# Half of w2 in a wide expert block as float32 products instead of split float32r products

## The chip, the cores and the metric

One Trainium2 chip, one core of it. The metric is the time of one execution in device microseconds. The kernel is the whole trunk in one launch; its inputs lie in HBM, and its output is written back there.

## The reference

Two layers. Each has a mixer (pooling and convolution groups), a normalization, a channel mixer, a normalization and a gated embedding. The first layer's channel mixer is a dense SwiGLU; the second's is a mixture of eight experts, of which each token takes two. The change is in that second one:

```python
def swiglu(h, w1, w3, w2):
    return (jax.nn.silu(h @ w1) * (h @ w3)) @ w2
...
    for e in range(N_EXPERTS):
        out = out + gates[:, e:e + 1] * swiglu(t, w1[e], w3[e], w2[e])
```

256 tokens, width 1024, 3584 hidden units an expert, all float32.

## The kernel before, in words

**Precision.** The products are made from float32r numbers, which hold fewer bits. A weight w is split into H (a cast of w to float32r, on ACT, line 146) and L (w - H, on DVE, line 161); the data likewise into h and l. `mm` (lines 342 to 352) then makes three products, h x H (347), h x L (351) and l x H (352), in one PSUM accumulation. Four small matrices that are named in `DIRECT` (line 39) are multiplied as float32 without a split (344).

**Experts.** Each expert gathers its tokens into places: the four with most tokens ("wide", even numbers here) into 128, the other four ("narrow", odd numbers) into 64. In a narrow block h and l lie side by side in the 128 columns of the stationary operand, so two products (347, 349) do what takes three in a wide one, and a product with a shift matrix folds the two halves together (1052). An expert has seven blocks (e, c) of 512 hidden units. `BLOCKS` (line 75) lists the 56 blocks: four wide ones, then narrow and wide in turns, then four narrow ones.

**A block** in `experts` (1054 to 1138) multiplies its w1 (1070) and w3 (1084), makes the gate product g on DVE (661), and then multiplies w2 of the block before it (`down`, 1105), whose hidden units were ready. At its end a wide block turns its own g: four transposes on PE (335), a cast to gH on ACT (320) and the rest gL on DVE (321). A narrow block's g is turned in the next block, after w1 (382 for the rest).

**Weights.** w1, w3 and w2 of a block come as two transfers of 1 MB each ("halves"; 12 for a pair of blocks), issued by the SP queue (line 117). All raw halves, all H and all L lie in one pool of 19 buffers of 8 KB a partition. `Weights.advance` is called whenever PE's next half is asked for: it issues the transfers ahead, and the cast and subtraction of following halves, as long as at most `hl` = 8 buffers hold H and L that are not used up. So a cast needs two buffers, and waits for whoever used these before: a subtraction that read a raw half, or a product that read an H or an L. The order of instructions on each engine is the order in which the program writes them (manual schedule); nothing overtakes on ACT and DVE.

**Around it.** Where a wide or narrow expert ends, its sums are evacuated and scattered to the tokens (814 to 817); where one begins, its tokens are gathered (796). In block 53 a branch on the counts of tokens (1039) is passed, which every engine waits at.

The names in the pair of blocks that the text follows, in the order in which PE multiplies them: N1 to N4 are the halves of w1 and w3 of the narrow block, W1 and W2 the halves of w2 of the wide block before it, A1 to A4 the halves of w1 and w3 of the wide block, B1 and B2 those of w2 of the narrow block.

Of the kernel before, what the change touches and what calls it, by code (L numbers as in the profile page):

```python
# [10 lines left out]
F32R = mybir.dt.float32r  # L11
# [6 lines left out]
P = 128  # L18
D = 1024
# [58 lines left out]
class Weights:  # L78
# [8 lines left out]
        self.slow, self.later = set(), []  # L87
        self.temps = TEMPS_START

    def add(self, name, src, k, n, whole=False):  # L90

        direct = name in DIRECT
        m = k if direct or whole else 1024 // n
        for j in range(0, k, m):
            self.names.setdefault(name, []).append(len(self.items))
            self.items.append(dict(load=len(self.loads), at=j * n, k=m, n=n, direct=direct, done=False,
                                   slots=2 if whole else 1))
        self.loads.append((src, k * n))

    def slot(self, n, dt=F32):  # L100
# [96 lines left out]
def trunk(ctx: ExitStack, tc: tile.TileContext, a: dict, out: bass.AP):  # L197
    nc = tc.nc
# [20 lines left out]
        return ap.tile([P] + shape, dt, tag=tag, name=tag)  # L219

    W = Weights(nc, wp)
    eids, at_place = [None], {}

    def expert_at(s):
# [5 lines left out]
    for l in range(L):  # L230
        for b in range(2):
            W.add(f"wg{b}{l}", a["w_gv"][l, 0, b], KD, 256)
            W.add(f"wv{b}{l}", a["w_gv"][l, 1, b], KD, 256)
        for k in range(2):
            W.add(f"wu{l}", a["w_u"][l, :, k * 2048:(k + 1) * 2048], 4, 512)
        for c in range(2):
            W.add(f"wo0{l}", a["w_out"][l, c, :, 0:2048], 4, 512)
        W.add(f"pw{l}", a["w_small"][l, :, 0:2048], 4, 512)
        for c in range(2):
            W.add(f"wo1{l}", a["w_out"][l, c, :, 2048:4096], 4, 512)  # L240

        def up_items(tag, w1, w3, nf, whole=False):
            for t, src in (("w1", w1), ("w3", w3)):
                for b in range(0, KD * nf, 2048):
                    W.add(f"{t}{tag}", piece(src, b), 2048 // nf, nf, whole)

        def down_items(tag, w2, nf, whole=False):
            for b in range(0, nf // P * D, 2048):
                W.add(f"w2{tag}", piece(w2, b), 2, D, whole)

        def piece(src, b):
            if callable(src):
                return lambda: src()[:, b:b + 2048]
            return src[:, b:b + 2048]

        def expert(name, e, c):

            if e == 0:
                return a[name][0, c]
            return lambda: a[name][bass.ds(expert_at(e), 1), c].rearrange("o p f -> (o p) f")  # L260

        if l % 2 == 0:
            units = [(f"d{c}", a["dense_w1"][c], a["dense_w3"][c], a["dense_w2"][c], nf, False)
                     for c, (f0, nf) in enumerate(DENSE_CHUNKS)]
        else:
            units = [(f"e{e}_{c}", *(expert(name, e, c) for name in ("exp_w1", "exp_w3", "exp_w2")), 512, (e, c) != (0, 0))
                     for e, c in BLOCKS]
        for i, (tag, w1, w3, w2, nf, whole) in enumerate(units):
            up_items(tag, w1, w3, nf, whole)
            if i:  # L270
                down_items(units[i - 1][0], *units[i - 1][3:])
        down_items(units[-1][0], *units[-1][3:])
        W.add(f"ple{l}", a["ple_w"][l], 2, D)
        for c in range(2):
            for b in range(2):
                W.add(f"gate{c}{l}", a["ple_gate_w"][l, c, :, b * 2048:(b + 1) * 2048], 4, 512)
# [41 lines left out]
    def split_into(dst, src):  # L318

        nc.scalar.copy(dst.h, src)  # L320
        nc.vector.tensor_sub(dst.l, src, dst.h.bitcast(F32))  # L321
        if dst.f is not None:
            nc.scalar.copy(dst.f, src)
# [8 lines left out]
    def transposes(src, n):  # L332
        t = mmt("tr")
        for i in range(n):
            nc.tensor.transpose(t[:, i * P:(i + 1) * P], src[:, i * P:(i + 1) * P], ident)
        return bank(t, n)
# [327 lines left out]
    def hidden(g, nf, h, tags=("gH", "gL")):  # L664

        n = nf // P
        gT = Split(*(tl(f"{t}{h}", [4, P], F32R) for t in tags))
        split_into(gT[:, :n, :], transposes(g, n))
        return gT

    def hidden_narrow(g, par):
# [372 lines left out]
    def experts(ranks, gates, xr, yacc, nxt, first, more, end):  # L1044

        prev = pend = made = turn = None
        selTs, state = [nxt[0], None], {0: nxt[1:]}

        def fold(p, lo):
            nc.tensor.matmul(p, shift, lo, start=False, stop=True, skip_group_check=True)

        for i, (e, c) in enumerate(BLOCKS):
            if i == 0:
                continue
            gsl, xg = state[e]
            par = e % 2
            narrow = PLACES[e] != P
            assert narrow == (par == 1)  # L1060
            if c == 0 or i == 1:
                accs = acc("y", 2 * par), acc("y", 2 * par + 1)
                state[e, "accs"] = accs
            accs = state[e, "accs"]
            lo = tl("xL1", [2, 512], F32R) if narrow else None
            p1 = mmt("p1")
            final = i == len(BLOCKS) - 1
            if final:
                W.cap = W.names[f"w2e{prev[0]}_{prev[1]}"][1]
            both(f"w1e{e}_{c}", [p1], [xg])  # L1070
            if made is not None:
                prev[3] = made()
                made = None
            if i == 1:
                prev = [0, 0, accs, first()]
            if narrow:
                nc.scalar.copy(lo[:, 0], p1)
            else:
                s_ = silu(p1, 512, par)
            more_ = c == 3 and e + 1 < NE  # L1080
            if more_:
                xg1 = gather(sel, xr, 1 - par, (0,), None, PLACES[e + 1])
            p3 = mmt("p3")
            both(f"w3e{e}_{c}", [p3], [xg])
            if narrow:
                nc.scalar.copy(lo[:, 1], p3)
                fold(p1, lo[:, 0])
                s_ = silu(p1, 512, par)
            else:
                g = glu(s_, p3, 512, par, gsl)  # L1090
            if more_:
                gather(sel, xr, 1 - par, (1,), xg1, PLACES[e + 1])
                state[e + 1] = gate_select(sel, cc, 1 - par), xg1
            pe, pc, paccs, pgT = prev
            ids = W.names[f"w2e{pe}_{pc}"]
            if final:
                down(ids[:1], paccs, pgT, pc == 0, False, True)
                if narrow:
                    fold(p3, lo[:, 1])
                    g = glu(s_, p3, 512, par, gsl)  # L1100
                W.cap = W.names[f"w2e{e}_{c}"][-1] + 1
                W.hl = HL_PRE
                down(ids[1:], paccs, pgT, False, pc == FE - 1, True, 2)
            else:
                down(ids, paccs, pgT, pc == 0, pc == FE - 1, True)
                if narrow:
                    fold(p3, lo[:, 1])
                    g = glu(s_, p3, 512, par, gsl)
            if turn is not None:
                if pend is not None:  # L1110
                    scatter(*pend, yacc, 2 * (turn % 2))
                    pend = None
                selTs[turn % 2] = turn_select(sel, turn % 2)
                turn = None
            elif pend is not None:
                scatter(*pend, yacc, 0)
                pend = None
            if pc == FE - 1:
                pend = selTs[pe % 2], evacuate(paccs)
            if more_:  # L1120
                turn = e + 1
            prev = [e, c, accs, None]
            if not narrow:
                prev[3] = hidden(g, 512, par)
            elif final:
                prev[3] = hidden_narrow(g, par)
            else:
                made = lambda g=g, par=par: hidden_narrow(g, par)
            if i + 1 < len(BLOCKS):
                e1, c1 = BLOCKS[i + 1]  # L1130
                if c1 == 3 and e1 + 1 < NE:
                    sel, cc = select(e1 + 1, ranks, gates, 0, (e1 + 1) % 2, PLACES[e1 + 1])
            if i == MORE_AT:
                more()
            if i == len(BLOCKS) - 1 - FE:
                W.temps = TEMPS_END
            if e == NE - 1:
                end(c)
        pe, pc, paccs, pgT = prev
        down(W.names[f"w2e{pe}_{pc}"], paccs, pgT, False, True, True)  # L1140
        end(FE)
        y = evacuate(paccs)
        return lambda h: scatter(selTs[1], y, yacc, 2 * (pe % 2), (h,))
# [166 lines left out]
```

## Time and profile before

| | |
|---|---|
| median of 3 runs | 1419.0 us (1416.77 to 1420.04) |
| profiled execution | 1417.34 us |
| its span, first to last instruction | 1415.6 us |
| mean granted clock of TensorE | 0.974 |
| PE, DVE, ACT, POOL busy | 1310.6, 1199.9, 938.9, 92.3 us |
| HBM read | 430.85 MB, 305 GB/s over the span |

Busy times are of instructions on each engine; PE's matmuls are pipelined, so that a duration of 0.39 us is longer than the step from one start to the next, and steps are read from starts. An idle time in brackets stands before the row's instruction, with what ended it.

### The profile page before, as it was taken

The page shows a single profiled execution, that of the slowest core. Times are in us where ns is not written, and L with a number is a line of the kernel's source. Part 1 is how long each engine was busy: PE and PEld are TensorE (multiplying, and loading weights), DVE is VectorE, ACT ScalarE, POOL GpSimd, SP SyncE. Part 2 cuts the span into 40 slices and gives each one's busy share as a digit, 9 for nine tenths or more (in the row PEclk, how much of TensorE's full clock was granted, in tenths as well). Part 3 has the DMA queues.
Part 4 walks back from the last instruction along what each step waited for, and adds up shares of the span by engine and source line. Part 5 has one row for each costly group of instructions (what it writes and reads, how often), then busy time and mean ns, then how long its engine had stood idle before and what let it go on. Part 6 is the DMA issues. An engine that isn't in the chain of part 4 may idle for free. (4 is left out here: it accounts for less than half of the span.)

```text
span 1415.6 us, 16882 instructions
## 1 busy us (share of the span) xinstructions
PE 1310.6 (93%) x6186; PEld 1060.0 (75%) x6186; DVE 1199.9 (85%) x1082; ACT 938.9 (66%) x883; POOL 92.3 (7%) x71
## 2 busy tenths in 40 slices
PE   6769999999869999999999999999999999999877
PEld 5638888888637887777777778778777777778656
DVE  3996844557966889999999999999999999999885
ACT  4543634426533668887887787787787788788662
POOL 0430000010560200000000000000000000000000
PEclk8889999999988999999999999999999999999999
DMA  9335755427544589999999999999999999999950
GB/s 381 121 119 178 266 180 179 178 97 272 196 173 177 204 334 406 420 387 350 418 417 354 402 420 353 391 417 367 384 421 376 375 409 387 371 360 423 356 191 30
DMA packets 62170, 433.07 MB, mean 306 GB/s; under 512 B 6960, under 2 KB 7472, under 8 KB 11008
## 3 DMA queue, kind: packets, MB, share of 16 engines
q1 hardware_dynamic: 60336, 425.60, 77.0%
q0 software_dynamic: 1168, 4.23, 0.9%
q10 hardware_dynamic: 576, 2.10, 0.5%
q8 instruction: 50, 0.82, 0.2%
q14 instruction: 40, 0.33, 0.1%
HBM read 430.85 MB, written 1.05 MB: 305 GB/s over the span
## 5 line engine op out<-in xcount | busy, mean ns | idle before, releaser
L161 DVE TENSOR_TENSOR w<-w 128x2048 fp32r<-128x2048 f32 (+1 forms) x460 | 895.9, 1988 | 72.6 <-ACT w L146 61.7
L146 ACT CAST w<-w 128x2048 fp32r<-128x2048 f32 (+1 forms) x460 | 751.1, 1671 | 157.1 <-PE p L351 39.5
L347 PE MATMUL p<-w,xH 128*128 128x512 f32 (+1 forms) x1096 | 434.5, 396 | 8.8 <-DVEq L1039 5.8
L352 PE MATMUL p<-w,xL 128*128 128x512 f32 (+1 forms) x648 | 251.0, 387 | 1.3 <-DVE xL L321 1.3
L351 PE MATMUL p<-w,xH 128*128 128x512 f32 (+1 forms) x648 | 250.3, 386 | 0.4 <-DVE w L161 0.4
L347 PEld LDWEIGHTS p<-w,xH 128*128 128x128 f32 x1096 | 207.8, 190 | 50.3 <-issue 6.5
L349 PE MATMUL p<-w,xH 128*128 128x512 f32 x448 | 180.3, 402 | 16.6 <-DVE w L161 16.6
L347 PE MATMUL y<-w,gH 128*128 128x512 f32 x448 | 176.4, 394 | 1.8 <-DVE gH L382 1.6
L352 PEld LDWEIGHTS p<-w,xL 128*128 128x128 f32 x648 | 122.5, 189 | 26.7 <-DVE xL L321 1.8
L351 PEld LDWEIGHTS p<-w,xH 128*128 128x128 f32 x648 | 122.7, 189 | 24.8 <-DVE w L161 1.3
L349 PEld LDWEIGHTS p<-w,xH 128*128 128x128 f32 x448 | 85.0, 190 | 46.8 <-DVE w L161 30.7
L347 PEld LDWEIGHTS y<-w,gH 128*128 128x128 f32 x448 | 84.6, 189 | 21.0 <-DVE gH L382 2.7
L490 DVE SCALAR_TENSOR_TENSOR yc<-w,vec,yc 128x256 f32<-128x256 f32 x156 | 91.8, 661 | 0.0
L349 PE MATMUL y<-w,gH 128*128 128x512 f32 x224 | 88.4, 395 | 2.4 <-DVE w L161 2.4
L351 PE MATMUL y<-w,gH 128*128 128x512 f32 x224 | 89.7, 400 | 0.0
L352 PE MATMUL y<-w,gL 128*128 128x512 f32 x224 | 87.4, 390 | 0.0
L498 POOL TENSOR_TENSOR gH<-gH,w 128x512 f32<-128x512 f32 x38 | 66.3, 1744 | 107.9 <-ACT w L495 105.5
L429 POOL DMA_DIRECT2D w<-in_pT x2 | 1.2, 580 | 984.6 <-DVE w L161 826.2
L652 ACT ACTIVATE s<-p 128x512 f32<-128x512 f32 (+1 forms) x69 | 41.0, 596 | 28.5 <-PE p L352 28.5
L321 DVE TENSOR_TENSOR gL<-tr,gH 128x512 fp32r<-128x512 f32 x38 | 25.6, 684 | 32.6 <-ACT gH L320 32.6
L351 PEld LDWEIGHTS y<-w,gH 128*128 128x128 f32 x224 | 42.0, 188 | 14.1 <-DVE w L161 6.0
L349 PEld LDWEIGHTS y<-w,gH 128*128 128x128 f32 x224 | 42.6, 190 | 11.7 <-DVE w L161 3.0
(223 smaller groups left out, 1454.2 us busy)
## 6 DMA issues: line engine op xcount, KB each, us to landing
w<-in_exp_w SPq DMA_DIRECT2D x336, 1024.0 KB, 8.0
w<-in_dense_w SPq DMA_DIRECT2D x33, 1024.0 KB, 5.1
w<-in_w_out SPq DMA_DIRECT2D x8, 1024.0 KB, 6.5
w<-in_ple_gate_w SPq DMA_DIRECT2D x8, 1024.0 KB, 5.3
w<-in_w_gv SPq DMA_DIRECT2D x6, 1024.0 KB, 6.1
w<-in_w_u SPq DMA_DIRECT2D x4, 1024.0 KB, 9.6
w<-in_w_gv SPq DMA_DIRECT2D x4, 512.0 KB, 6.9
w<-in_w_small SPq DMA_DIRECT2D x2, 1024.0 KB, 10.2
```

The lines of the kernel that those rows point to most:

```text
L146: nc.scalar.copy(h, w)
L161: engine.tensor_tensor(l, w, h.bitcast(F32), op=ALU.subtract)
L321: nc.vector.tensor_sub(dst.l, src, dst.h.bitcast(F32))
L347: nc.tensor.matmul(ps, x.h, wh, start=start, stop=False)
L349: nc.tensor.matmul(ps, x.h, wl, start=False, stop=stop)
L351: nc.tensor.matmul(ps, x.h, wl, start=False, stop=False)
L352: nc.tensor.matmul(ps, x.l, wh, start=False, stop=stop)
L429: nc.gpsimd.dma_start(pT.f, a["pT"][l])
L490: nc.vector.scalar_tensor_tensor(yc[:, ct], src, w1, yc[:, ct], op0=ALU.mult, op1=ALU.add)
L498: nc.gpsimd.tensor_tensor(part[b], part[b], p, op=ALU.add)
L652: nc.scalar.activation(s_[:, :nf], p1[:, :nf], AF.Silu)
```

## The change

In the blocks of wide experts, but for the very first block (0, 0), the first half of w2 (W1 above) is neither cast nor subtracted. It stays in its raw buffer until PE multiplies it as float32: one product in place of three, for each of its two slices of 128 hidden units and each of the two halves of 512 output columns. There are 27 such blocks. The hidden units are laid out accordingly (`hidden_direct`): the first 256 as float32 in a tile of their own, on ACT, the other 256 as h and l as before. The raw buffer counts as one buffer of a direct half (`live(True)`) and no longer as two of `hl`.

```diff
-    def add(self, name, src, k, n, whole=False):
+    def add(self, name, src, k, n, whole=False, direct=False):
-        direct = name in DIRECT
+        direct = direct or name in DIRECT
...
-                                   slots=2 if whole else 1))
+                                   slots=2 if whole and not direct else 1))
...
+    def whole_w2(e, c):
+        return PLACES[e] == P and (e, c) != (0, 0)
...
-        def down_items(tag, w2, nf, whole=False):
-            for b in range(0, nf // P * D, 2048):
-                W.add(f"w2{tag}", piece(w2, b), 2, D, whole)
+        def down_items(tag, w2, nf, whole=False, direct=0):
+            for n, b in enumerate(range(0, nf // P * D, 2048)):
+                W.add(f"w2{tag}", piece(w2, b), 2, D, whole, n < direct)
...
+    def hidden_direct(g, par):
+        h, l = (tl(f"{t}{par}", [4, P], F32R) for t in ("gH", "gL"))
+        gT = Split(h, l, tl("gL1", [4, P]))
+        ps = transposes(g, 4)
+        nc.scalar.copy(gT.f[:, :2], ps[:, :2])
+        split_into(Split(h[:, 2:], l[:, 2:]), ps[:, 2:])
+        return gT
...
-                prev[3] = hidden(g, 512, par)
+                prev[3] = hidden_direct(g, par)
```

The change also moves instructions. DVE, one pair of blocks in the first narrow and the second wide expert (w are weights, gL the rest of a wide block's hidden units, g a gate product, gH in the row of 128x4x64 that of a narrow block). Before:

```order
L321 TENSOR_TENSOR gL_5176<-tr,gH_5175 128x512
L161 TENSOR_TENSOR w<-w 128x2048 x6
L661 SCALAR_TENSOR_TENSOR g_5285<-p_5215,gsl_3924,s_5246 128x512
L161 TENSOR_TENSOR w<-w 128x2048 x2
L382 TENSOR_TENSOR gH_5324<-tr,gH_5324 128x4x64
L161 TENSOR_TENSOR w<-w 128x2048 x2
L661 SCALAR_TENSOR_TENSOR g_5371<-p_5334,gsl_4765,s_5332 128x512
L161 TENSOR_TENSOR w<-w 128x2048 x2
```

With the change (its lines are numbered some seven higher):

```order
L328 TENSOR_TENSOR gL_5106<-tr,gH_5105 128x256
L161 TENSOR_TENSOR w<-w 128x2048 x5
L668 SCALAR_TENSOR_TENSOR g_5205<-p_5147,gsl_3916,s_5178 128x512
L161 TENSOR_TENSOR w<-w 128x2048 x2
L389 TENSOR_TENSOR gH_5244<-tr,gH_5244 128x4x64
L161 TENSOR_TENSOR w<-w 128x2048 x2
L668 SCALAR_TENSOR_TENSOR g_5291<-p_5254,gsl_4717,s_5252 128x512
L161 TENSOR_TENSOR w<-w 128x2048 x2
```

One subtraction of the six after gL is gone, and gL is half as long; the rest stands where it stood. The last two rows of L161 before the wide block's g (661, 668) are those of B2 and N1, the two after it those of N2 and N3.

ACT in the same pair, with the semaphores that an instruction waits for (DMAHW a transfer, DVE and PE a count of that engine). Before, the casts are A3, A4, B1, then B2, N1, N2, N3:

```order
L146 CAST w_5268<-w_5109 128x2048 [waits DMAHW7_49,DVE_49,PE_49]
L146 CAST w_5290<-w_5127 128x2048 [waits DMAHW0_49,DVE_49,PE_49]
L146 CAST w_5308<-w_5147 128x2048 [waits DMAHW1_49,DVE_49,PE_49]
L381 CAST gH1_5324<-tr_5325 128x4x64 [waits PE_49]
L652 ACTIVATE s0_5332<-p1_5287 128x512
L146 CAST w_5337<-w_5161 128x2048 [waits DMAHW2_49,DVE_49]
L146 CAST w_5355<-w_5186 128x2048 [waits DMAHW3_49,DVE_49]
L146 CAST w_5375<-w_5200 128x2048 [waits DMAHW4_49,PE_49]
L146 CAST w_5389<-w_5216 128x2048 [waits DMAHW5_49,DVE_49,PE_49]
L320 CAST gH0_5401<-tr_5403 128x512 [waits PE_49]
```

With the change, the same casts:

```order
L146 CAST w_5182<-w_5039 128x2048 [waits DMAHW7_49,DMAHW3_49,PE_49]
L146 CAST w_5210<-w_5057 128x2048 [waits DMAHW0_49,DVE_49]
L146 CAST w_5228<-w_5077 128x2048 [waits DMAHW1_49,DVE_49]
L388 CAST gH1_5244<-tr_5245 128x4x64 [waits PE_49]
L659 ACTIVATE s0_5252<-p1_5207 128x512
L146 CAST w_5257<-w_5091 128x2048 [waits DMAHW2_49,PE_49]
L146 CAST w_5275<-w_5118 128x2048 [waits DMAHW3_49,DVE_49,PE_49]
L146 CAST w_5295<-w_5124 128x2048 [waits DMAHW4_49,DVE_49,PE_49]
L146 CAST w_5309<-w_5148 128x2048 [waits DMAHW5_49,DVE_49,PE_49]
L683 COPY gL1_5323<-tr_5324 128x256 [waits PE_49]
L327 CAST gH0_5321<-tr_5324 128x256
```

A4 and B1, which waited for PE, wait for DVE alone; B2 and N1, which waited for DVE alone, wait for PE. By the values of the semaphores B2 waits for the last h x L product of A3, and N1 for the last one of A4.

## Rows read from the trace of the kernel before

**Rows 1.** The page: busy time by engine; the experts' transfers (count, KB each, us to landing).

```profile
PE 1310.6 (93%) x6186; PEld 1060.0 (75%) x6186; DVE 1199.9 (85%) x1082; ACT 938.9 (66%) x883; POOL 92.3 (7%) x71
...
w<-in_exp_w SPq DMA_DIRECT2D x336, 1024.0 KB, 8.0
```

**Rows 2.** Busy us by stretch: length, PE, PEld, DVE, ACT, POOL, clock, DMA share, GB/s.

```profile
524.00:1331.00 807.00, 775.87 (x3545) 624.05 (x3543) 767.90 (x501) 650.61 (x489) 0.62 (x1) 1.00 0.98 389
688.10:718.40 30.30, 29.61 (x132) 23.42 (x131) 29.23 (x17) 25.21 (x19) 0.00 (x0) 1.00 1.01 419
...
1260.00:1331.00 71.00, 63.77 (x281) 50.27 (x279) 70.70 (x44) 59.74 (x45) 0.62 (x1) 0.99 0.96 390
```

**Rows 3.** Timeline of PE: first and last product of B1, B2; transposes; N1's first products.

```profile
713.84 0.39 PE L347 MATMUL y<-w,gH 128*128 128x512 f32 x1
...
717.24 0.39 PE L349 MATMUL y<-w,gH 128*128 128x512 f32 x1
717.62 0.66 PE L335 MATMUL tr<-con,g 128*128 128x128 f32 x4
718.03 0.48 PE L347 MATMUL p<-w,xH 128*128 128x512 f32 x1
```

**Rows 4.** Groups from 524 to 1331 us: busy us, mean ns | idle us before, releasers.

```profile
L161 DVE TENSOR_TENSOR w<-w 128x2048 fp32r<-128x2048 f32 x302 | 680.4, 2287 | 39.0 <-ACT w L146 30.8 <-PE y L351 2.5 <-DMA w<-in_exp_w 2.5
L146 ACT CAST w<-w 128x2048 fp32r<-128x2048 f32 x304 | 573.1, 1914 | 120.2 <-PE p L351 36.0 <-PE y L347 23.4 <-PE y L351 21.1
...
L321 DVE TENSOR_TENSOR gL<-tr,gH 128x512 fp32r<-128x512 f32 x25 | 17.1, 683 | 0.0
...
L382 DVE TENSOR_TENSOR gH<-tr,gH 128x256 fp32r<-128x256 f32 x25 | 10.5, 418 | 0.0
```

**Rows 5.** Timelines of DVE, then PE, from B2's subtraction to W1's products.

```profile
716.82 0.74 DVE L661 SCALAR_TENSOR_TENSOR g<-p,gsl,s 128x512 f32<-128x512 f32 x1
717.57 4.49 DVE L161 TENSOR_TENSOR w<-w 128x2048 fp32r<-128x2048 f32 x2
721.99 0.69 DVE L321 TENSOR_TENSOR gL<-tr,gH 128x512 fp32r<-128x512 f32 x1
...
723.87 0.40 PE L347 MATMUL p<-w,xH 128*128 128x512 f32 x1
724.92 0.50 PE L349 MATMUL p<-w,xH 128*128 128x512 f32 x1 [0.66 <-DVE w L161]
...
727.13 0.50 PE L351 MATMUL y<-w,gH 128*128 128x512 f32 x1
727.46 0.39 PE L352 MATMUL y<-w,gL 128*128 128x512 f32 x1
```

**Rows 6.** Timeline of PE: float32 products of the mixer in layer 0.

```profile
72.36 10.46 PE L344 MATMUL ps_o<-w,cat 128*128 128x512 f32 x24
```

**Rows 7.** Waits from 524 to 1331 us: in total, times, longest.

```profile
PEld y L351 <- DVE w L161: 6.0, 21, 0.3
...
ACT w L146 <- DMA w<-in_exp_w: 3.7, 4, 1.0
```

**Rows 8.** Timelines of ACT, DVE, PE in the pair from 815 us, around N1's cast.

```profile
840.71 5.53 ACT L146 CAST w<-w 128x2048 fp32r<-128x2048 f32 x3 [1.43 <-PE p L351]
...
842.66 2.29 DVE L161 TENSOR_TENSOR w<-w 128x2048 fp32r<-128x2048 f32 x1 [1.06 <-ACT w L146]
844.87 0.74 DVE L661 SCALAR_TENSOR_TENSOR g<-p,gsl,s 128x512 f32<-128x512 f32 x1
...
845.67 0.66 PE L335 MATMUL tr<-con,g 128*128 128x128 f32 x4 [1.14 <-DVE g L661]
```

**Rows 9.** Timeline of PE: half of a gather.

```profile
738.61 1.95 PE L796 MATMUL ps_xg<-m,xr 128*128 128x128 f32 x16
```

**Rows 10.** Timelines of DVE and PE before the branch.

```profile
1328.46 2.47 DVE L817 TENSOR_TENSOR w<-w,ps_sc 128x512 f32<-128x512 f32 x4
...
1331.13 0.77 PE L347 MATMUL p<-w,xH 128*128 128x512 f32 x1 [5.83 <-DVEq L1039]
```

More of the change, by code (lines that the diff above doesn't have):

```diff
@@ L262, in trunk @@
         if l % 2 == 0:
-            units = [(f"d{c}", a["dense_w1"][c], a["dense_w3"][c], a["dense_w2"][c], nf, False)
+            units = [(f"d{c}", a["dense_w1"][c], a["dense_w3"][c], a["dense_w2"][c], nf, False, 0)
                      for c, (f0, nf) in enumerate(DENSE_CHUNKS)]
         else:
-            units = [(f"e{e}_{c}", *(expert(name, e, c) for name in ("exp_w1", "exp_w3", "exp_w2")), 512, (e, c) != (0, 0))
+            units = [(f"e{e}_{c}", *(expert(name, e, c) for name in ("exp_w1", "exp_w3", "exp_w2")), 512, (e, c) != (0, 0),
+                      1 if whole_w2(e, c) else 0)
                      for e, c in BLOCKS]
-        for i, (tag, w1, w3, w2, nf, whole) in enumerate(units):
+        for i, (tag, w1, w3, w2, nf, whole, _) in enumerate(units):
             up_items(tag, w1, w3, nf, whole)
```

## The prediction

> **What bounds the kernel now.** I read the page first: over the span TensorE (PE) is busy 93%, VectorE (DVE) 85%, ScalarE (ACT) 66% [rows 1]. That is a mean over unlike stages, so I cut out the stretch that the change touches, the experts' alternating blocks up to the branch behind them (524 to 1331 us). There PE is busy 776 of 807 us, DVE 768, ACT 651, at full clock (granted 1.00, the 2.4 GHz level), and the DMA engines are 0.98 busy at 389 GB/s [rows 2]. Three resources are nearly full, so the page cannot say which one sets the pace; a pair of blocks has to be walked.
>
> Names: in a pair, PE multiplies the halves N1 to N4 (w1 and w3 of the narrow block, two products a slice), then W1 and W2 (w2 of the wide block before it, three products), then A1 to A4 (w1, w3 of the wide block, three products), then B1 and B2 (w2 of the narrow block, two). Before the change each of the twelve halves is cast by ACT (L146) and subtracted by DVE (L161); the change takes W1 out.
>
> PE's pitch: sixteen products of B1 and B2 start from 713.84 to 717.24, fifteen steps of 0.227 us; four transposes take 0.41 [rows 3]. A pair without other work is 120 products, 2 folds and 8 transposes: 27.2 + 0.5 + 0.8 = 28.5 us. The pair from 688.1 to 718.35 takes 30.25, so 1.75 us a pair is lost in waits. DVE has 29.2 busy in the same 30.3 us, but over the stretch its subtractions also stood 30.8 us waiting for ACT's casts, which in turn wait for PE to release a buffer. So neither engine is simply the bound: it is a **ring** of PE, buffer, cast (1.91), subtraction (2.29) and PE again [rows 2, 4]. PE falls behind mostly at N4: the row at 724.92 starts 1.05 after the product before it, 0.82 late, because DVE ran two subtractions, the half-tile of the hidden units (L321, 0.69) and then N4's [rows 5].
>
> **Part by part.** *The products.* W1 loses 12 products and gets 4 of float32. The trace has float32 products with 512 columns: 24 records at L344 in 10.46 us, that is (10.46 - 0.59)/23 = 0.429 each, weight loads between them included. Sixteen such products a layer are in the code and 64 records in all, so one product is two records, 0.858 us [rows 6]. A half costs 4 x 0.858 = 3.43 instead of 12 x 0.227 = 2.72: **+0.71 us of PE** in each of 27 wide blocks, **+19.2**. All of it is on PE's path, which has no free stretch of that size after W1. The Trainium skill (FP8 and Floating Point Precision, TensorE Precision Notes) counts four passes for true float32 against the three here; at 0.227 a pass that would be 0.907 a product and +24.5 in place of +19.2. The measured pitch stands, and 24.5 is not needed further.
>
> *DVE and ACT.* Each block saves a cast (1.91 of ACT), a subtraction (2.29 of DVE), and half of gL: 683 falls to about 418 ns, the time of the 256-column L382, 0.27 less [rows 4]. ACT makes two copies of half a tile instead of one of a whole; the one start more is hidden, since ACT is idle a fifth of the stretch and 1.91 is taken from it. What does this relief give PE? (a) W1's own wait: PE's weight loads waited 21 times, 6.0 us in all, for a subtraction at L351 [rows 7]; but the row at 727.13 is followed at 727.46, a pitch of 0.33, so it costs 0.11 each: **-2.3** [rows 5]. (b) N4's wait shrinks by the shorter gL ahead of it, 0.27 in eleven pairs and by my walk 0.12 in ten: **-4.2**. It does not vanish: N4's cast may start only when N1 is multiplied, and 1.91 + 2.29 = 4.2 after that is later than N2 and N3 are done (3.6). (c) Three gathers wait for the selection, queued behind gL: 0.27 each, **-0.8**. The rest of the freed DVE time falls into the wide part, where DVE already stops for buffers.
>
> *A new wait.* This is the place I weigh most. N1's cast stands in front of the wide block's gate product on DVE (order: two subtractions, L661, two subtractions), and PE's transposes wait for that product. Before, N1's cast waits in most pairs for a DVE release alone; after, in 16 of the pairs it waits for PE too (the order of ACT shows it; by the semaphore's counts the awaited product is the last low-half product of A4). Three of these had it before already, and the trace prices it: in the pair from 815, the cast waits 1.43 and starts at 840.71, the subtraction at 842.66, the gate at 844.87, the transposes at 845.67 with 1.14 idle [rows 8]. Without the wait L661 runs at 716.82 and the transposes at 717.62, only 0.15 late [rows 3, 5]. The pair is 31.4 long instead of 30.25: +1.15. Three more have half a gather's products between A4 and the transposes; a half is 16 records in 1.95 us [rows 9], enough cover. Ten are left: **+11.5**. Bounds: 0, if the buffer comes free sooner, and 13.0. I take the pair's measured difference.
>
> *The end of the stretch.* From 1260 to 1331 DVE is busy 70.7 of 71 us and ends in four adds (L817); a branch then lets PE go at 1331.13 after 5.83 idle [rows 2, 10]. Here two subtractions and two half gL less, about 4.9 us, are really on the path. PE's scatter, which feeds the adds, moves 1.4 later, so the branch comes about 3.5 sooner, where the sum above had +1.4: **-4.9**.
>
> *DMA.* The same 336 transfers. A float32 half stays in its buffer until it is multiplied, but casts waited for a transfer only 3.7 us in all [rows 7]; I cost it at nothing, bounds -1 to +3. SP and POOL keep their order.
>
> Sum: 19.2 - 2.3 - 4.2 - 0.8 + 11.5 - 4.9 = **+18.5 us**. The profiled execution took 1417.34 (span 1415.6), 1.7 below the median of 1419.0, so the sum gives 1435.8 by it and 1437.5 by the median. I say 1436.
>
> **Rivals.** *DVE is the bound, and the relief pays (faster).* For it: DVE is 95% busy in the stretch and loses 8% of its work. The Trainium skill (Perfetto Trace Analysis, Identifying the Most-Contended Engine) says to judge VectorE by occupancy and TensorE not by matmul time but by weight loads; by that DVE at 95% comes before PE at 77% (624 of 807), and this change would be right. The pitch of 0.227 with no gap through most of a pair speaks against it. As a mechanism: if all waits at N3, N4, W1 and the transposes went, a pair would fall to 28.5 + 0.7 = 29.2; but a pair also needs twelve transfers of 1024 KB [rows 1], 12.6 MB, which at the 419 GB/s of this pair take 30.0, at a DMA share of 1.01 [rows 2]. So a plain pair gains at most 0.25, fourteen of them 3.5; the ten with gathers or scatters, where the DMA has room, at most 1.75 - 0.71 = 1.0 each, 10; the end 3.5; the three blocks at the front lose 2. That is -15, 1402. It decides as soon as more than 0.71 of the 1.75 lost in a pair goes.
>
> *No new wait.* The casts are late but the gate is not: if N1's buffer is released one half sooner, 11.5 drops out: +7, 1424. For it: ACT and DVE both have spare time now and a different start of a pair could shift the ring. Against: the awaited product stands four transposes and sixteen products before the point of need, and 3.63 us cannot cover 1.91 + 2.29 + 0.74.
>
> *More waits.* B2's cast now waits for A3 as well, and N2 to N4 shift with the late gate. If PE loses another 0.5 in sixteen pairs: +8, 1444.
>
> That the change does not do what it says is no rival: the order has 27 subtractions fewer.
>
> **How the numbers follow.** Main case 0.57 (1428 to 1443: float32 fixed, new wait 0.7 to 1.3, end -2 to -7); no new wait 0.18; more waits 0.13; faster 0.12. A measurement of this kernel tells some 0.2%, 2.8 us, from no change. Only the lower edge of "no new wait" falls within that: same 0.05, faster 0.12, slower 0.83. The range leaves out the faster case and the far end of the slow one: 1419 to 1447.
>
> **What would show it.** Right: 216 new float32 records of the experts' w2 at 0.429 pitch; DVE's busy time down by 60 to 70 us with PE idle more, not less; transposes (L335's counterpart) waiting for the gate some 13 times at 1.1; the pair near 31.6 to 31.9; the branch's idle below 4. Wrong: a pair at 30 or less, no wait at the transposes, or float32 products off 0.858.

## The result and the profile after

| | before | after |
|---|---|---|
| median | 1418.13 us (4 runs) | 1441.61 us (4 runs, 1440.97 to 1443.87) |
| profiled execution, its span | 1417.34, 1415.6 | 1440.98, 1439.2 |
| ratio, 95% interval | | 1.0167 [1.0150, 1.0185] |

The change costs 23.5 us; 18.5 were forecast (1436, range 1419 to 1447). In the code of after the lines up to 670 stand seven higher, the later ones sixteen: 354, 356, 358, 359 are the four products of `mm`, 351 the float32 product, 342 the transposes, 668 the gate product, 328 and 389 the rests gL and gH.

The page (busy time by engine), then the stretch of the experts (length, PE, PEld, DVE, ACT, POOL, clock, DMA share, GB/s), which answers to [rows 1, 2]:

```profile
PE 1326.1 (92%) x6078; PEld 1042.6 (72%) x6078; DVE 1135.1 (79%) x1055; ACT 891.8 (62%) x883; POOL 92.4 (6%) x71
```

```profile
524.00:1331.00 807.00, 774.43 (x3368) 593.24 (x3368) 684.26 (x459) 588.35 (x474) 0.00 (x0) 1.00 0.96 379
```

DVE lost 65 us of work over the span, ACT 47, and PE is no busier in the stretch than it was: 774 us against 776, with more float32 to do. The clock is granted in full in both. So the freed time of DVE and ACT did not become pace; they stand waiting. The waits from 524 us to the branch (engine, line, waited for: us in total, times, longest) show where, beside [rows 7] and the 30.8 us of DVE's wait. First two lines of before:

```profile
PE p L349 <- DVE w L161: 16.6, 21, 1.7
...
PE tr L335 <- DVE g L661: 3.4, 3, 1.1
```

After:

```profile
DVE w L161 <- ACT w L146: 90.9, 78, 3.7
...
PEld y L351 <- issue: 37.4, 156, 0.2
...
PEld p L356 <- DVE w L161: 28.2, 41, 2.0
...
PE tr L342 <- DVE g L668: 14.9, 13, 1.1
...
PE p L356 <- DVE w L161: 13.0, 19, 1.6
...
PE p L354 <- DVEq L1055: 5.7, 1, 5.7
```

Before, PE's transposes waited for the gate 3 times, 3.4 us in all; now 13 times. The wait of W1's products for a subtraction is gone, and the one of N's second products (L356) fell only from 16.6 us in 21 to 13.0 in 19. The branch lets PE go after 5.7, as before [rows 10].

W1 and W2 of one block, in PE's timeline (start, length, instruction):

```profile
733.36 0.39 PE L1068 MATMUL p<-xL,shift 128*128 128x512 f32 x1
733.59 3.60 PE L351 MATMUL y<-w,gL 128*128 128x512 f32 x8
736.62 0.80 PE L354 MATMUL y<-w,gH 128*128 128x512 f32 x1
737.26 0.39 PE L358 MATMUL y<-w,gH 128*128 128x512 f32 x1
...
739.55 0.39 PE L359 MATMUL y<-w,gL 128*128 128x512 f32 x1
739.78 0.40 PE L1068 MATMUL p<-xL,shift 128*128 128x512 f32 x1
```

Eight records are four float32 products. From 733.59 to the fold at 739.78 it is 6.19 us, where 24 products of 0.227 would take 5.45: +0.74 a block, with 0.71 forecast.

The new wait in a plain pair, in the timelines of ACT, DVE and PE; it answers row for row to [rows 8]:

```profile
719.74 5.53 ACT L146 CAST w<-w 128x2048 fp32r<-128x2048 f32 x3 [0.81 <-PE p L358]
```

```profile
721.69 2.29 DVE L161 TENSOR_TENSOR w<-w 128x2048 fp32r<-128x2048 f32 x1 [0.43 <-ACT w L146]
723.90 0.74 DVE L668 SCALAR_TENSOR_TENSOR g<-p,gsl,s 128x512 f32<-128x512 f32 x1
```

```profile
724.70 0.66 PE L342 MATMUL tr<-con,g 128*128 128x128 f32 x4 [1.14 <-DVE g L668]
```

The cast of N1 waits for a product of A4, the subtraction follows 1.95 later, the gate 2.21 after that, the transposes 0.80 later, 1.14 late: the spacing of [rows 8] to 0.02 us, now in a pair that had none of it.

**Where the 23.6 us between the two spans went**, by the length of each pair (from N1's first product to the next N1's, read from PE's timeline): ten pairs with a new gate wait +13.8; three pairs behind the gather in a wide block +6.3 (32.45 to 34.53 each); nine others, float32 less the relief, +2.4; the last two pairs and the narrow block behind them +1.0; the block of the branch, up to its release of PE, -2.2 (21.82 to 19.63); ahead of the first pair +0.9, behind the branch +1.3.

In one of the three pairs behind the gather in a wide block, which starts at 759.45, PE's rows of after read:

```profile
767.47 0.50 PE L356 MATMUL p<-w,xH 128*128 128x512 f32 x1 [1.61 <-DVE w L161]
```

It is N4's wait of [rows 5], 0.66 there, 1.61 here; in the same pair of before it is 0.52. N4's subtraction stands on DVE behind those of N2 and N3, and these come late. N2's cast in ACT's timeline, before (the pair starts at 752.17) and after:

```profile
748.14 3.72 ACT L146 CAST w<-w 128x2048 fp32r<-128x2048 f32 x2
```

```profile
757.24 3.74 ACT L146 CAST w<-w 128x2048 fp32r<-128x2048 f32 x2 [1.71 <-PE y L354]
```

It starts 4.03 ahead of N1's first product before, 2.21 ahead after, since it now waits for a product of the narrow block's w2.

### The profile page after: what moved, and what is told of

It reads as the page before. It is cut to its first block, busy times and chain, and to the rows that moved or that the text cites. A ratio compares the mean times of both kernels' runs of the same rounds, so it can differ in the third digit from the quotient of the medians.

```text
span 1439.2 us, 16618 instructions
## 1 busy us (share of the span) xinstructions
PE 1326.1 (92%) x6078; PEld 1042.6 (72%) x6078; DVE 1135.1 (79%) x1055; ACT 891.8 (62%) x883; POOL 92.4 (6%) x71
## 5 line engine op out<-in xcount | busy, mean ns | idle before, releaser
L161 DVE TENSOR_TENSOR w<-w 128x2048 fp32r<-128x2048 f32 (+1 forms) x433 | 836.2, 1969 | 152.4 <-ACT w L146 121.8
L146 ACT CAST w<-w 128x2048 fp32r<-128x2048 f32 (+1 forms) x433 | 698.3, 1656 | 164.2 <-PE p L358 46.0
L356 PE MATMUL p<-w,xH 128*128 128x512 f32 x448 | 180.1, 402 | 13.6 <-DVE w L161 13.0
L354 PE MATMUL y<-w,gH 128*128 128x512 f32 x340 | 145.0, 427 | 2.8 <-DVE gH L389 2.6
L356 PEld LDWEIGHTS p<-w,xH 128*128 128x128 f32 x448 | 84.7, 189 | 44.4 <-DVE w L161 28.5
L351 PE MATMUL y<-w,gL 128*128 128x512 f32 x216 | 97.5, 594 | 0.0
L356 PE MATMUL y<-w,gH 128*128 128x512 f32 x224 | 88.4, 394 | 2.4 <-DVE w L161 2.4
L354 PEld LDWEIGHTS y<-w,gH 128*128 128x128 f32 x340 | 64.5, 190 | 22.8 <-issue 6.5
L351 PEld LDWEIGHTS y<-w,gL 128*128 128x128 f32 x216 | 40.6, 190 | 40.7 <-issue 38.8
L659 ACT ACTIVATE s<-p 128x512 f32<-128x512 f32 (+1 forms) x69 | 41.0, 597 | 29.2 <-PE p L359 29.2
L342 PE MATMUL tr<-con,g 128*128 128x128 f32 x268 | 40.3, 275 | 15.9 <-DVE g L668 15.9
L342 PEld LDWEIGHTS tr<-con,g 128*128 128x128 f32 x268 | 31.9, 141 | 27.8 <-DVE g L668 21.7
L388 ACT CAST gH<-tr 128x256 fp32r<-128x256 f32 x28 | 10.4, 373 | 66.8 <-PE tr L342 66.7
```

The lines of the kernel that those rows point to most:

```text
L146: nc.scalar.copy(h, w)
L161: engine.tensor_tensor(l, w, h.bitcast(F32), op=ALU.subtract)
L351: nc.tensor.matmul(ps, x.f, it["F"][cols], start=start, stop=stop)
L354: nc.tensor.matmul(ps, x.h, wh, start=start, stop=False)
L356: nc.tensor.matmul(ps, x.h, wl, start=False, stop=stop)
L388: nc.scalar.copy(dst[:, :, :H], src[:, :, :H])
```

## The experiments

**Theory:** PE's path through a pair sets the pace; the change lengthens it by the float32 products and by the late gate. **Rivals:** DVE or the transfers bound the pair, and the products hide; or the gate is only where the time shows, and the ring of buffers as a whole is short, so that the time returns elsewhere when that wait goes. The kernel before, run beside them, had 1417.1 to 1417.5 in each set.

**e1_three_of_four**, after with a quarter of the float32 products left out, so that PE's time for W1 is 2.57 us against 2.72 before:

```diff
                 for c in range(2):
+                    if it["direct"] and j and c:
+                        continue
                     mm(accs[c], gT[:, at, :], it, ...
```

> The changed kernel with one of the four float32 products of each half left out (second slice, second 512 columns), so that part of the expert sums is missing. Main theory (float32 time lies on PE's path in full): 27 x 0.858 = 23 us less than the changed kernel's 1441.6, so 1417 to 1422; the waits for the gate product (13 of about 1.1) stay. Rival (PE has slack and the ring of buffers sets the pace): less than 10 us less, 1432 or more, with longer waits in the same pairs.

Measured: 1426.97 (1424.13 to 1427.25), ratio 1.0059 [1.0042, 1.0076]: 14.6 of 23.2 us came back, between the two. The plain pair gave back all of it, 31.61 to 30.77, and so did the pairs that hold a gather (36.98 to 36.17, 34.33 to 33.48); the six behind them did not (31.96 to 32.16, 34.53 to 35.05; one of them, 33.82 long, also lost 1.7 to a fall of the clock, last section). There the edit moved more than PE's time: around the gathers some casts wait for other releases than in after, and in the three pairs behind the gather in a wide block the cast ahead of the gate now waits 2.60 us for a product of A4, where in after it did not wait. So the gate wait stands in 16 places, these three and the 13:

```profile
PE tr L342 <- DVE g L668: 18.3, 16, 1.1
PE p L356 <- DVE w L161: 16.2, 19, 2.0
```

The kernel is thus still 9.9 us slower than before, with 4 us less of PE's time, but a part of that is what the edit itself moved. The plain pair is clean: 30.77 against 30.25 before. The new order costs by itself, and on this ring less work on DVE and ACT does not make up for it.

**e2_gate_first**, after with N1's subtraction issued behind the wide gate product:

```diff
+            W.hold = hold and n == len(ids) - 1
...
-                if rest == "later":
+                if rest == "later" or self.hold:
...
-            both(f"w3e{e}_{c}", [p3], [xg])
+            both(f"w3e{e}_{c}", [p3], [xg], not narrow)
...
                 g = glu(s_, p3, 512, par, gsl)
+                W.rests(nc.vector)
```

> The changed kernel with N1's subtraction issued on DVE behind the wide block's gate product instead of ahead of it; casts, buffers and products as they were. Main theory (the gate product is late because it queues behind a subtraction whose cast waits for A4): the 13 waits of the transposes for the gate go, of about 1.15 each; N1 to N4 are then subtracted later and give back 0.3 to 0.5 a pair, so 8 to 12 less than 1441.6, 1430 to 1434. Rival (the wait is only where another shortage shows, PE is set by float32 and DMA): the waits move to N1 to N4 in full, within 3 us of 1441.6.

Measured: 1434.98 (1434.75 to 1439.56), 1.0132 [1.0111, 1.0153]. No wait for the gate is left in the trace, but 6.6 us came back of the 14.9 that PE had stood there. The rest moved to the weight loads of N (products are L357 here):

```profile
PEld p L357 <- DVE w L162: 41.7, 69, 2.0
PE p L357 <- DVE w L162: 13.4, 21, 1.6
```

41.7 in 69 against 28.2 in 41. In a plain pair the fold and the products of N take 9.31 in place of 8.48, where the gate had cost 1.3. Plain pairs are 0.55 shorter, those with a gather 0.8 to 0.9 longer. An idle time at one place is not the price of that place.

**e4_before_gate_first**, the same edit in the kernel before:

> The kernel before with one edit: in a wide block the subtraction of N1 stands behind the gate product. Before, only three places wait for that gate, 1.1 each (3.4 us). If the wait is worth what it is long: -2 to -4, 1413 to 1416, with the plain pair at 30.25. Rival (as in e2_gate_first, the subtraction behind the gate is late at the narrow halves, so that it is not the gate alone that the ring is short of): no gain or slower, 1417 to 1424, the plain pair longer than 30.25.

Measured: 1417.17 (10 runs), 0.9997 [0.9987, 1.0006]: nothing, as the rival had it, though not where it had it: the plain pair is no longer than before. Three pairs of 31.4 fell to 30.28, and three of 36.6 rose to 37.28. N's second products wait 17.2 us in place of 16.6.

**e6_before_more_products**, the kernel before with three more float32r products in W1 of each wide block, and no cast, subtraction or transfer more or less:

```diff
+                    for _ in range(more if n == j == c == 0 else 0):
+                        nc.tensor.matmul(accs[0], gT.h[:, 0, :], it["H"][:, 0, 0:512], start=False, stop=False)
```

> The kernel before with three more float32r products of 512 columns in W1 of each of the 27 wide blocks, 3 x 0.227 = 0.68 us of PE a pair (about what float32 adds, 0.71), with nothing moved on any queue, no cast and no subtraction taken away. The sum that they add to the output is left in. If PE's path is what sets the pace and each microsecond of it counts in full: 27 x 0.68 = +18.4, 1435 (1432 to 1438), the plain pair 30.25 -> 30.9. If DVE or the ring of buffers bounds the pair and PE's own time hides in its waits: under +8, 1425 or less, with N4's wait shrinking by what is added. In between if the waits at N4 take a part of it.

Measured: 1436.16 (1434.64 to 1438.92), 1.0129 [1.0102, 1.0157]: +18.6, all of it as far as the interval tells (14 to 22). Only three pairs behind a gather hid a part (31.01 to 31.20), as N4's wait there shrank. One plain pair (columns as above) shows that nothing else moved in it: 30.25 became 30.93, with DVE's 29.2 us of [rows 2]:

```profile
693.18:724.11 30.93, 30.25 (x134) 23.94 (x133) 29.17 (x17) 25.14 (x19) 0.00 (x0) 1.00 1.01 416
```

DVE does not bound the kernel before, though it is busy 95% of the stretch: its waits grow with PE's path. The first rival falls with it, on this ring.

**e3_hl10** and **e5_before_hl10**, after and before with ten buffers for halves not yet used up, in place of eight:

```diff
-HL_START, HL_PRE, HL_FIRST, HL_SECOND, HL_MOE = 8, 12, 8, 6, 8
+HL_START, HL_PRE, HL_FIRST, HL_SECOND, HL_MOE = 8, 12, 8, 6, 10
```

> The changed kernel with 10 instead of 8 buffers for prepared halves in the experts and so two fewer for transfers ahead. Main theory (late releases of buffers make the waits): every cast's release stands one half earlier in PE's order, N1's is A3 instead of A4 and N4's B2 instead of N1, so the waits at the gate and at N4 go; a plain pair falls from 31.6 to its products, 28.5 + 0.7, or to the 30.0 that its transfers take at 419 GB/s: 1.6 to 2.2 a pair, 38 to 50 in all, 1392 to 1404. Rival (the transfers or PE's own time set the pace already): 1430 or more.

> The kernel before with the same 10 instead of 8 buffers. Main theory (ring of releases): the wait at N4 goes; the pair falls from 30.25 to the larger of DVE's 29.2 and the transfers' 30.0: 0.3 to 0.9 a pair in 24 pairs and 0.5 to 1 in those with gathers, 1400 to 1411. Rival (DVE, at 95%, is simply full): within 4 us of 1418. Against the changed kernel with 10 buffers: if transfers set the pace in both, the two agree within 6 us; if DVE does, the changed one is the faster.

Measured: after 1426.02 (1423.82 to 1429.26), 1.0066 [1.0048, 1.0083]; before **1393.36** (1393.17 to 1394.39), 0.9830 [0.9813, 0.9846], with e8 the fastest here of the kernels that compute the whole. Both expectations missed: before gained more than expected, after only 15.6. The waits of e3, and of e5 (product lines as before):

```profile
PEld tr L342 <- DVE g L668: 25.0, 16, 1.6
PE tr L342 <- DVE g L668: 18.3, 16, 1.1
```

```profile
PEld tr L335 <- DVE g L661: 14.3, 18, 1.6
PE tr L335 <- DVE g L661: 6.7, 8, 1.1
```

In both, PE's waits for a subtraction at N (L356, L349) are gone: with two buffers more the casts come early enough. In e3 the gate wait stays in 16 places, because the deeper window also moves the casts one half ahead in the program; by the order and the counts of the semaphores the half ahead of the gate is now N2, and its cast waits for A4 as N1's did. On the longer ring the change thus costs more than on the short one, 32.7 us (e3 against e5). A plain pair of e5, 28.84 us, has PE and DVE without a gap, and 421 GB/s; here DVE may be the bound, which no run tells:

```profile
685.15:713.99 28.84, 28.84 (x131) 23.60 (x130) 28.81 (x17) 24.87 (x19) 0.00 (x0) 1.00 1.01 421
```

**e7_hl10_gate_first** and **e8_before_hl10_gate_first** have both edits, in after and in before. They tell the gate from the ring: e2 removed the gate wait on a short ring, e7 removes it on a longer one.

> The changed kernel with ten buffers of held halves instead of eight (as in e3_hl10) and the subtraction ahead of the wide gate product put behind it (as in e2_gate_first). In e3_hl10 nothing but the gate wait was left, 16 x 1.30 = 20.9 us. Main theory (the gate wait is the second cost of the change): the gate waits go and with a deeper window no wait at N3 or N4 comes back; -15 to -21 from 1426, 1405 to 1411, the plain pair 30.7 -> 29.5 to 29.8. Rival (there is slack nowhere in the ring, a wait taken away at the gate comes back at the narrow halves, as in e2_gate_first): 1420 or more, with L357's waits for a subtraction at 10 us or more.

> The kernel before with both edits. e5_before_hl10 (1393.4) had 11 gate waits of 0.78 left, 8.6 us in all. Main theory: they go, -4 to -8.6, 1385 to 1389; and e7_hl10_gate_first less this one is the float32 products alone, 17 to 22 us. Rival (the subtraction behind the gate comes late at N2 or N3): 1393 or more.

Measured: e7 1403.74 (1402.87 to 1405.15), 0.9897 [0.9873, 0.9922], 22.3 less than e3 by the medians, 19.9 by the profiled executions: the 20.9 us at the gate (PE's steps in the 16 places, 1.30 late each, of which the row of e3 shows 18.3 as idle) went in full, and no wait at N came back. Only the wait for the selection, in the three pairs whose narrow block holds a gather, grew from 0.89 to 1.73 each. e8 1394.54 (1390.28 to 1398.92), 0.9841 [0.9802, 0.9879]: with e5 no difference that this measurement tells, and less steady (last section). Between the two medians lie 9.2 us, between the two profiled executions 13.0, where 17 to 22 were expected for float32 alone: e8's pair is not at PE's own 28.5, so the change still has some relief to give there. By plain pairs e7 stands 0.64 above e8, 29.37 against 28.73, and its block of the branch is 2.5 shorter (20.27 against 22.78). PE has no gap in e7's:

```profile
688.25:717.62 29.37, 29.37 (x127) 22.94 (x126) 26.49 (x17) 23.41 (x19) 0.00 (x0) 1.00 0.98 403
```

**e11_deep_gate_three_of_four**, e7 with the edit of e1:

> e7_hl10_gate_first (1403.7) with one of the four float32 products of each half left out, 0.858 less of PE in each of the 27 wide blocks; that part is missing in the output. PE's time for the half is then 2.57, about the 2.72 of twelve split products, so this is the relief of ACT and DVE alone on a ring that is not short. If PE's path sets the pace there (29.37 a pair): -23.2 in full, 1380 to 1384, the plain pair 28.5, and then the relief is worth some 8 to 10 against the kernel before with the same two edits (1390 to 1394). If the ring or the transfers take it up, as in e1_three_of_four where -14.6 of -23.2 came through: 1387 or more, the plain pair 28.8 or more.

Measured: 1383.36 (1383.02 to 1384.01), 0.9756 [0.9735, 0.9776]: 20.4 of 23.2 came back, where e1 got 14.6. The plain pair:

```profile
688.61:717.14 28.53, 28.53 (x126) 22.58 (x125) 26.29 (x16) 23.30 (x20) 0.00 (x0) 1.00 1.01 421
```

PE has no gap in it. On a ring that is not short, this kernel is 10 us faster than e5 (1383.4 against 1393.4), but not all of that is the relief of DVE and ACT: PE has 0.15 less to do in each of the 27 blocks, 4 us by the pitches, and e5 lacks the edit at the gate. So some 6 us are left for the relief and that edit together, an estimate; float32 at its real price costs 20.4.

**e9_before_hl12**, before with twelve:

> The kernel before with twelve buffers of held halves instead of eight: seven of the nineteen are left for raw halves. If what e5_before_hl10 gained (-23.7) came from the depth of the ring, it is nearly used up at ten, since the plain pair there is 28.85 and 28.5 is PE's own time: 1388 to 1396. If raw halves become short, casts wait for transfers (ACT's wait for DMA, 3.7 us before) and it is slower than 1396.

Measured: 1397.86 (1396.03 to 1401.84), 0.9851 [0.9826, 0.9876]: no better than ten. Its plain pairs are as long as e5's (28.85). What it loses lies elsewhere: in the profiled execution, the longest of its four, the first pair starts 8.0 us later (538.76 against 530.75), with the clock granted at 0.95 from 460 to 524 us where e5 has 1.00, and its block of the branch is 24.42 long against 22.66. Of the 8.0, 3.2 are there in layer 0 already, 139 us into the span (142.40 against 139.21 for the same product), ahead of all that the constant acts on. Why the rest was lost was not looked into.

## Why the prediction was right, and where its steps failed

- **The products, +19.2: right.** One float32 product is two records at 0.429. Per block it is +0.74 where it can be read, and PE's path takes nearly all of it: e6 (+18.6 for 18.4 added) shows it in before's ring, the plain pair of e1 (-0.84 for 0.86) in after's, e11 (-20.4 for 23.2 taken away) in the longer one. The Trainium skill (FP8 and Floating Point Precision, TensorE Precision Notes) counts four passes for true float32. At the pitch here that is an estimate of 0.907 a product, and of 3.85 us for the eight records and one split product behind them. They took 3.67 here, from 733.59 to 737.26, which less one step of 0.227 is 0.86 a product. The measured pitch decides, as in the prediction.
- **The new wait, +11.5: right where it shows.** 13 waits at 1.1, 16 places with the dependence, three covered by a gather; the ten pairs grew by 13.8 us, where the forecast had 11.5 for the gate and, by its terms, some 4 for float32 less the relief. What the prediction did not have: the figure is the idle time at the gate, not what removing it brings. In after's ring that is 6.6 (e2), in before's nothing (e4), and only with two buffers more the full amount (e7).
- **W1's wait, -2.3: right. N4's, -4.2: right in size by luck.** Neither PE nor its weight loads wait for a subtraction at L351. PE's waits for a subtraction at N's second products fell by 3.6 us in all (16.6 to 13.0), but that is 6.9 less elsewhere and 3.3 more in the three pairs of the next point, where the prediction had less everywhere.
- **The gathers' wait for the selection, -0.8: right.** It fell from 1.15 to 0.89 in each of the three pairs.
- **Pairs behind the gather in a wide block: the step that failed.** The prediction had no term of their own for these three: by its sum float32 less a shorter wait at N4, about +0.4 each, an estimate from its terms. They grew by 2.1 each, some 5 us more than forecast, as much as the whole miss; the other misses, of both signs, nearly cancel. N2's cast there waits for a product of the narrow block's w2 (the row at 757.24), so that N4's subtraction, behind N2's and N3's on DVE, is late and PE waits 1.6 in place of 0.5. The prediction named such waits under "more waits" and put them at the wrong pairs. e3 to e7 show what of it is the ring's and what the gate's: 34.53 in after, where these pairs have no gate wait, 34.57 with the edit at the gate (e2), 33.53 with the deeper ring, which takes the wait at N4 away and brings one at the gate (e3), 32.20 with both (e7), against 31.48 in e5 and e8. The 0.72 that are left are what float32 adds. The order inside such a pair was not tried by itself.
- **The end, -4.9: too large.** From the start of the last pair to the release by the branch it is 1.9 us less (64.93 to 63.04), not 3.5: DVE, busy 64.5 us of it before, now works 59.3 and stands 3.7. The branch's idle time did not fall below 4: it is 5.7.
- **"The relief pays": it fell here, and for a reason that the prediction gave only in part.** The prediction bounded this rival by transfers, twelve of 1024 KB at 419 GB/s or 30.0 us a pair. That bound was wrong: plain pairs run at 28.84 in e5 and 28.53 in e11, still at 421 GB/s. The rate holds; but transfers run ahead, and what a short pair does not load, a long one with a gather does (in e11 one of 37.01 us at 420 GB/s). A floor of 30.0 can hold only for the mean of a whole expert's pairs. What kept the relief from paying was the ring: DVE, though 95% busy, did not set the length of a pair (e6).
- The Trainium skill (Perfetto Trace Analysis, Identifying the Most-Contended Engine) says to optimize first the engine of the highest occupancy. Between VectorE and TensorE in the kernel before that is VectorE by its measure, and taking 8% of its work away, at the price of 0.7 us of TensorE a block, made the kernel 1.7% slower. The same page (Optimization Strategy) says that a gap which repeats on the engine that should be saturated can mean too few buffers; e5 agrees: 1.75 us were lost in each plain pair of before, and two buffers more gave 23.7 us.

In sum, of the 23.5 us about 19 are float32's price, and the rest is what the new order adds on a ring that was already short, less what the relief gives back. That the sum came within 5 us is in part luck, since the terms at N4, at the end and behind the gathers missed in both directions. Two buffers more do not mend it by themselves: the change then costs 32.7 (e3 against e5). With the subtraction also behind the gate product it costs 10.4 (e7 against e5).

## What to carry to other kernels

When three resources are each over 90% busy, here PE, DVE and the DMA engines, do not ask which one bounds; follow one buffer round, from the product that frees it to the product that needs it, and see whether that round is longer than the time in between. Here work taken off an engine on such a ring paid little until the ring had slack, so try a buffer more before a change of arithmetic: one constant was worth 23.7 us here, the change of arithmetic cost 23.5. Try it in the kernel as it is and in the changed one: the same constant gave the changed kernel only 15.6. And an idle time in front of an instruction prices that instruction only if nothing else on the ring is close behind; take it away on the chip before it is put into a sum.

## What the runs showed of the hardware

A short idle time of PE can bring the clock down, and does not always. In e8, PE waits 1.86 us for the selection in three pairs. In PE's timeline at two of them:

```profile
840.08 2.12 PE L799 MATMUL ps_xg<-m,xr 128*128 128x128 f32 x16 [1.85 <-DVE cc L768]
```

```profile
1056.60 3.51 PE L799 MATMUL ps_xg<-m,xr 128*128 128x128 f32 x16 [1.86 <-DVE cc L768]
1059.76 0.77 PE L348 MATMUL p<-w,xH 128*128 128x512 f32 x1
```

After the same idle time the sixteen small products take 2.12 us once and 3.51 the other time. The granted clock there (third column from the right) is near 0.5, the level of 1.2 GHz, and back at 1.00 some 4 us later:

```profile
1057.00:1059.00 2.00, 2.00 (x11) 2.00 (x11) 2.00 (x2) 0.16 (x1) 0.00 (x0) 0.52 1.00 418
1059.00:1061.00 2.00, 2.00 (x10) 1.82 (x9) 2.00 (x2) 0.85 (x2) 0.00 (x0) 0.63 1.01 414
1061.00:1063.00 2.00, 2.00 (x11) 1.63 (x10) 1.26 (x3) 2.00 (x2) 0.00 (x0) 1.00 1.03 422
```

That pair is 38.89 long where its likes are 37.27. e1 shows a second fall: behind a wait of 1.93 at N4 (from 1120.46 to 1122.39) the granted clock is 0.50 from 1124 to 1126 us, and the pair is 33.82 long, where its two likes, with waits of 1.96 and 1.95, are 32.16 and 32.15. In the kernel before, the wait for the selection is 1.15 and the longest at N4 1.7, and no pair of it shows such a fall. Such falls may be why e8's four times lie between 1390 and 1399, at mean clocks from 0.971 down to 0.965; that is not shown.

And a start behind a change of form is not the pitch. The eighth float32 record starts at 736.60 ((3.60 - 0.59)/7 = 0.43 a step), the first split product is shown 0.02 later, and its successor 0.64 after that instead of 0.227 (736.62 to 737.26 above). Read from the first start to the next row alone, a float32 product would seem to cost 0.76; only a row further on gives its 0.86.
